# A hybrid attention and MLP block on one core: the bias rows of all 24 heads go to scratch in one DMA with 16 copies each, and a Toeplitz tile is read back by eight DMAs of 16 partitions

## The chip, the cores and the metric

The kernel runs on one core of one Trainium2 chip. The metric is device microseconds of one execution. The kernel before was timed three times: 1610.1, 1610.7 and 1612.06 us, median 1610.7 us.

The core has five engines that run their own instruction streams in order: PE (matmul), DVE (vector), ACT (activation), POOL (GpSimd) and SP, which here only issues DMAs. Sixteen DMA engines move data. Transfers that SP issues appear in the trace as queue q1, those that POOL issues as queue q0.

## The reference, cut to what matters

One decoder layer on 256 tokens of width 2048, all in float32: an RMS norm, one projection of 11,800 columns, three attention mixers A, B and C of eight heads each, a gated sum of their projections, an output projection, and an MLP of width 8192. What the change touches is the relative position bias that every mixer adds to its logits:

```python
def t5_bucket(dist):
    n = jnp.maximum(dist, 0)
    exact = N_BUCKETS // 2
    log_ratio = jnp.log(jnp.maximum(n, 1).astype(jnp.float32) / exact) / math.log(BUCKET_MAX_DIST / exact)
    large = jnp.minimum(exact + (log_ratio * (N_BUCKETS - exact)).astype(jnp.int32), N_BUCKETS - 1)
    return jnp.where(n < exact, n, large)
...
    dist = (jnp.arange(BAND_BLOCK)[:, None] + pad) - jnp.arange(span)[None, :]
    bias = jnp.transpose(bias_tbl[t5_bucket(dist)], (2, 0, 1)).reshape(n_kv, g, BAND_BLOCK, span)
    logits = logits + bias.astype(jnp.float32)
    ...
    p = masked_softmax(logits, mask, sink)
    out = jnp.einsum('bnkgql,bnlkd->bnqkgd', p.astype(v.dtype), vp)
```

The bias of a head depends on the distance query minus key alone. For a tile of 128 queries by 256 keys it is therefore a Toeplitz matrix: each row is the row above it, shifted by one column. All of it is in 383 numbers per head.

## The kernel before, in words

**Dense work.** All weights stream through the core once. `steps` is one list of pieces of weight, each piece 128 partitions by `a` by `b` floats (512 KB for most, 280 KB for the projection of 280 columns called `proj_vw`). For each step `load` issues a DMA from SP into a tile `raw`, `fetch` has ACT round it to `hi` (L79) and DVE take the rest `lo` (L80), and `mm` multiplies both with the activations on PE (L224 to L228 in `dmajor`, L251 to L253 in `tmajor`). The pool `ring` holds four buffers of each of `raw`, `hi` and `lo`.

**Order.** The order is written out by hand: the loop at the end of `hybrid_block` goes through the steps. At step j it runs the step's `pre`, then one slice of the side work in `tasks` (`advance`), then the previous step's evacuation (`late`), then `fetch(j + 3)`, and last the matmuls of step j. So PE has up to three fetched steps ahead of it. But DVE and ACT take their instructions in this order too: the side work of step j+1 stands on DVE behind the `lo` of step j+3, and PE's own side work (transposes, attention) stands between the matmuls of the steps.

**Bias.** `bias_rows`, a task that begins four steps before the end of `proj_vw`, makes `rm`, 24 partitions by 383 floats, one row per head, with the causal mask added. `spread_rows(m)` then writes the eight rows of mixer m into the DRAM tile `scr`, each row 128 times at a pitch of 384 floats (L195). `load_master(m, g)` reads four heads of it at a pitch of 383 floats, so that partition p starts p floats earlier in the row: that is the Toeplitz tile `master`, 128 partitions by 4 heads by 256 keys (L203). There is one buffer for `master`. POOL issues both kinds of DMA, in program order: a `master` load waits for the `scr` write behind it and for DVE's last read of the previous `master` (L450).

`spread_rows(0)` runs in `bias_rows`; `spread_rows(1)` and `spread_rows(2)` run in `start_attn`, when the steps of the first and second branch projection begin to be laid down in the program. POOL reaches them earlier than that place suggests, because it has little else to do. The tile `master` is first read by DVE in `attn_a` (L542, mixer A) and in `core` (L444, mixers B and C).

**Names in the rows.** `cT` and `cs` are a small transpose and its source in `finish`, the end of the block compression; `pt` and `P` are the transposed probabilities in `core`; `fold` is a small constant that POOL's queue copies at the start.

Of the kernel before, what the change touches and what calls it, by code (L numbers as in the profile page):

```python
# [8 lines left out]
F32 = mybir.dt.float32  # L9
# [12 lines left out]
SCALE = 128.0 ** -0.5  # L22
NB = 383
AHEAD = 3

# column offsets in w_in
AQ, AKC, AVC, AKS, AVS, AKW, AVW = 0, 1024, 1280, 1536, 1792, 2048, 2304
BQ, BK, BV = 2584, 3608, 3864
CQ, CK, CV = 4120, 5144, 5400
# [4 lines left out]
def hybrid_block(ctx: ExitStack, tc: tile.TileContext, x, w_in, cmp_pos, cmp_w1, cmp_w2, swa_sinks,  # L34
                 w_branch, w_out, w_mlp_in, w_mlp_out, norm_mix, norm_mlp, norm_final, rel_bias,
                 onehot, rmask, cmask, out):
    nc = tc.nc
# [17 lines left out]
    def pair(name="pair"):  # L55
        return psum.tile([128, 2, 512], F32, name=name, tag="mm")

    # ---------------------------------------------------------------- streamed weights
    steps = []
    tasks = []  # L60

# [3 lines left out]
    loaded = {}  # L65

    def load(j):
        src, a, b = steps[j][:3]
        loaded[j] = ring.tile([128, a, b], F32, name="raw", tag="raw")
        nc.sync.dma_start(loaded[j], src)  # L70

    def fetch(j):
# [19 lines left out]
        while any(t[0] == name for t in tasks):  # L92
            advance()

    # ---------------------------------------------------------------- constants
    xt = bigt([128, 2, D], F32, "xt")

    def load_x(c0, c1):
# [29 lines left out]
    hm = cst.tile([128, 4], F32, name="hm")  # L128
    nc.vector.tensor_reduce(hm, ident.rearrange("p (h c) -> p h c", h=4), axis=AX.X, op=OP.add)

    # ---------------------------------------------------------------- first norm
    part = cst.tile([128, 2, 4], F32, name="part")
    rs = cst.tile([128, 2], F32, name="rs")
    rsh = cst.tile([128, 2], F32, name="rsh")
# [2 lines left out]
    HT = [bigt([128, 8, 512], F32R, f"HT{i}") for i in range(2)]  # L137

    def split_scaled(tiles, k, src, g0):
        """hi and lo parts of two K tiles, src * gain, into columns 0:256 and 256:512."""  # L140
        d = [tiles[(k + a) // 8][:, (k + a) % 8] for a in range(2)]
        g = [gains[:, g0 + k + a:g0 + k + a + 1] for a in range(2)]
        for a in range(2):
            nc.scalar.activation(d[a][:, 0:256], src[:, a], AF.Copy, scale=g[a])
        for a in range(2):
            nc.vector.scalar_tensor_tensor(d[a][:, 256:512], src[:, a], g[a], d[a][:, 0:256].bitcast(F32),
                                           op0=OP.mult, op1=OP.subtract)
# [4 lines left out]
        nc.vector.tensor_copy(gains[:, c0:c0 + n], pc[:, 0:n])  # L152

    def x_block(i):
        """Two K tiles of x * gain; the row factor of the norm follows where products leave PSUM."""
        b = bank("xT").rearrange("p (a q) -> p a q", a=2)
        for a in range(2):
            k = 2 * i + a
            for tt in range(2):
                nc.tensor.transpose(b[:, a, tt * 128:(tt + 1) * 128], xt[:, tt, k * 128:(k + 1) * 128], ident)  # L160
        split_scaled(HT, 2 * i, b, 0)
# [22 lines left out]
    def bias_rows():  # L184
        pr = obank("pr")
        nc.tensor.matmul(pr[0:24, 0:NB], rb, oh, start=True, stop=True)
        nc.vector.tensor_tensor(rm, pr[0:24, 0:NB], rm, op=OP.add)
        yield
        spread_rows(0)
        load_master(0, 0)  # L190
        yield

    def spread_rows(m):
        """Row h 128 times at pitch 384; read at pitch 383 it is a Toeplitz matrix."""
        nc.gpsimd.dma_start(scr[m * 8:(m + 1) * 8, :, 0:NB],  # L195
                            rm[m * 8:(m + 1) * 8, None, :].to_broadcast([8, 128, NB]))

    scr = dram.tile([24, 128, 384], F32, name="scr")
    masters = {}

    def load_master(m, g):
        t = att.tile([128, 4, 256], F32, name="master")
        nc.gpsimd.dma_start(t, bass.AP(tensor=scr.tensor, offset=scr.offset + (m * 8 + g * 4) * 128 * 384 + 127,  # L203
                                       ap=[[383, 128], [128 * 384, 4], [1, 256]]))
        masters[m, g] = t

    # ---------------------------------------------------------------- dense jobs
    def dmajor(w, c0, rhs, evac, kts=KT, pre=None, cuts=(0, 4, 8, 12, 16)):
        """256 columns of w as [column, token]: weights stationary."""
        st = {}  # L210
        for k0, k1 in zip(cuts, cuts[1:]):
            src = w[k0 * 128:k1 * 128, c0:c0 + 256].rearrange("(k p) c -> p k c", p=128)

            def mm(hi, lo, k0=k0, k1=k1):
                if k0 == 0:
                    st["ps"] = pair()
                ps = st["ps"]
                for k in range(k1 - k0):
                    kt = k0 + k
                    r = rhs(kt)  # L220
                    for c in range(2):
                        cs = slice(c * 128, (c + 1) * 128)
                        if kt:
                            nc.tensor.matmul(ps[:, c, 0:256], lo[:, k, cs], r[:, 0:256],  # L224
                                             start=False, stop=False)
                        nc.tensor.matmul(ps[:, c, :], hi[:, k, cs], r, start=kt == 0, stop=kt == kts - 1)  # L226
                        if not kt:
                            nc.tensor.matmul(ps[:, c, 0:256], lo[:, k, cs], r[:, 0:256],  # L228
                                             start=False, stop=False)

            add(src, k1 - k0, 256, mm, pre if k0 == 0 else None,
                (lambda: evac(st["ps"])) if k1 == kts else None)

    def tmajor(w, c0, n, lhs, evac, kts=KT, kc=2, pre=None):
        """n columns of w as [token, column]: activations stationary."""
        st = {}
        for k0 in range(0, kts, kc):
            src = w[k0 * 128:(k0 + kc) * 128, c0:c0 + n].rearrange("(k p) c -> p k c", p=128)

            def mm(hi, lo, k0=k0):  # L240
                if k0 == 0:
                    st["ps"] = pair()
                ps = st["ps"]
                for k in range(kc):
                    kt = k0 + k
                    l = lhs(kt)
                    for tt in range(2):
                        o = ps[:, tt, 0:n]
                        lh = l[:, tt * 128:(tt + 1) * 128]
                        ll = l[:, 256 + tt * 128:256 + (tt + 1) * 128]  # L250
                        nc.tensor.matmul(o, lh, hi[:, k], start=kt == 0, stop=False)  # L251
                        nc.tensor.matmul(o, lh, lo[:, k], start=False, stop=False)  # L252
                        nc.tensor.matmul(o, ll, hi[:, k], start=False, stop=kt == kts - 1)  # L253

            add(src, kc, n, mm, pre if k0 == 0 else None,
                (lambda: evac(st["ps"])) if k0 + kc == kts else None)
# [19 lines left out]
        for tt in range(2):  # L276
            nc.scalar.activation(dst[:, tt], ps[:, tt, c0:c0 + n], func, scale=scale[:, tt:tt + 1])

    # ---------------------------------------------------------------- projections
    w = w_in[0]  # L280
    qT, kT, vt = {}, {}, {}

# [36 lines left out]
            tasks.append(("A", attn_a(1)))  # L319
        tmajor(w, AVW, 280, hT, ev, kc=2)  # L320

    # ---------------------------------------------------------------- compression of blocks
    XH = {}
    kcT = cst.tile([128, 30], F32, name="kcT")
    vcr = cst.tile([128, 2, 128], F32, name="vcr")
# [86 lines left out]
            nc.vector.tensor_copy(vcr, pk[:, 0:256].rearrange("p (g d) -> p g d", g=2))  # L412
        yield

    # ---------------------------------------------------------------- attention
    oT = {}

    def new_o(m):
# [1 line left out]
            oT[m] = bigt([128, 8, 512], F32R, "oT")  # L420

    def core(m, g, q, k, v, o, first, last, gate):
        """Causal attention of the four heads of one kv group; o accumulates [d, (head, token)]."""
        M = masters[m, g]
        h0 = 4 * g
        qp = att.tile([128, 2, 4, 128], F32R, name="qp", tag="P0")
# [154 lines left out]
        store_o(0, g, o)  # L581
        yield

    # ---------------------------------------------------------------- gates and branches
    gt = {}

    def gates(m):
# [26 lines left out]
            tmajor(w_branch[0, m], c * 512, 512, lambda kt: oT[m][:, kt], ev, kts=8, pre=pre)  # L614

    def to_dmajor(src, c, dst, gain0):
        """Column chunk c of a [token, column] tile, transposed and split into hi and lo parts."""
        if not dst:
            dst += [bigt([128, 8, 512], F32R, "dmaj") for _ in range(2)]
        for i in range(2):  # L620
# [12 lines left out]
                split_scaled(dst, k, b, gain0)  # L633
            yield

    # ---------------------------------------------------------------- output projection
    acc = {}
    H2 = []

# [34 lines left out]
        nc.vector.reciprocal(r2, r2)  # L674
        yield

    # ---------------------------------------------------------------- MLP
    hid = {}

    parts = [(4 * i, 4) for i in range(7)] + [(28, 3), (31, 1)]  # L680
# [27 lines left out]
    fin = {}  # L708

    def mlp_last(p):  # L710
        """The last K tiles: the first token tile is done before the second, from the same weights."""
        keep = []
        r0 = parts[p][0] * 256

# [68 lines left out]
            nc.scalar.dma_start(rows[:, 1280:2048], o[:, 1280:2048])  # L783
            nc.sync.dma_start(rows[:, 640:1280], o[:, 640:1280])

    # ---------------------------------------------------------------- order of the work
    def job(f, *a, **kw):
        """The steps of one dense job, taken off the list."""
        n = len(steps)
        f(*a, **kw)  # L790
        r = steps[n:]
        del steps[n:]
        return r
# [29 lines left out]
    n = len(steps)  # L823
# [9 lines left out]

    def start_attn(m, key):
        drain("ABC"[m - 1])
        spread_rows(m)
        load_master(m, 0)
        for g in range(2):
            tasks.append(("ABC"[m], attn(m, g, qT[m], kT[key], vt[key])))
# [12 lines left out]
    n = len(steps)  # L852
# [9 lines left out]
    mlp_last(len(parts) - 1)  # L862
    steps[n - 4] = before(steps[n - 4], load_nf)

    # ---------------------------------------------------------------- emission
    ready = {}
    load_x(0, 256)
    load(0)
# [17 lines left out]
    for j in range(len(steps)):  # L886
# [3 lines left out]
        advance()  # L890
        if late:
            late()
        if j + AHEAD < len(steps):
            ready[j + AHEAD] = fetch(j + AHEAD)
        mm(*ready.pop(j))
# [5 lines left out]


def _constants():
    """Distance buckets and causal masks of the two token tiles: they follow from the shapes alone."""
    import math
    import numpy as np
    dist = 255 - np.arange(NB)
# [28 lines left out]
```

## Time and profile before

| | |
|---|---|
| median of three runs | 1610.7 us (1610.1 to 1612.06) |
| profiled execution, span from first to last instruction | 1610.1 us |
[...]
| PE busy | 1534.5 us, 95% |
| DVE, ACT, POOL busy | 940.4, 718.8, 23.9 us |
| moved by all DMA queues | 298.16 MB, of which POOL's queue 9.33 MB |
| `scr` writes | 3 of 1532 KB, median 36.1 us from issue to landing |
| `master` loads | 6 of 512 KB, median 5.2 us from issue to landing |

PE is the engine that sets the time, so what counts is the time in which it is idle and the time in which it runs at a lower granted clock. The page's 40 slices of about 40 us show both: PE is at 9 tenths or more in most slices, and lower in the first and in slices 4, 7, 8 and 12; the clock line falls in slices 4, 8 and 12. No profile lists anything around the span; the span lies at the lower end of the three times.

### The profile page before, as it was taken

To read this page: it belongs to the slowest core of one execution; us is meant where nothing else is said; L and a number is where in the kernel's file an instruction comes from. 1 tells how busy PE (TensorE), PEld (TensorE's weight loads), DVE (VectorE), ACT (ScalarE), POOL (GpSimd) and SP (SyncE) were. 2 spreads that over 40 slices of the span, in tenths; PEclk is the share of its full clock that TensorE was granted. 3 is DMA by queue.
4 is the path that set the end of the run, shared out by engine and by line. 5 is a ranking of instruction groups with operands and counts; after the bars stand their busy time and mean duration, and the time that the engine had idled before them with its cause. 6 is when DMAs were issued, how large, how long until landed. Compare 5 with 4: busy or idle time off the path is not lost.

```text
span 1610.1 us, 20195 instructions
## 1 busy us (share of the span) xinstructions
PE 1534.5 (95%) x7878; PEld 1305.1 (81%) x7878; DVE 940.4 (58%) x1082; ACT 718.8 (45%) x942; POOL 23.9 (1%) x33
## 2 busy tenths in 40 slices
PE   8995997899959999999999999999999999999997
PEld 7894885688849888888888888888888888888885
DVE  5772663565637547744755666565655566555656
ACT  6551542455524445444445444343434444443443
POOL 1000000000000000000000000000000000000002
PEclk9997999899979999999999999999999999999999
DMA  8696756655666665566655656656565656566563
GB/s 248 193 276 110 223 158 126 174 169 173 176 138 172 183 194 187 168 183 192 225 187 184 188 177 197 192 190 190 186 195 188 193 181 198 181 198 194 189 218 118
DMA packets 211231, 298.16 MB, mean 185 GB/s; under 512 B 10268, under 2 KB 129612, under 8 KB 210752
## 3 DMA queue, kind: packets, MB, share of 16 engines
q1 hardware_dynamic: 207504, 287.15, 58.2%
q0 software_dynamic: 3456, 9.33, 3.8%
q8 instruction: 61, 1.00, 0.3%
q10 hardware_dynamic: 176, 0.40, 0.1%
q14 instruction: 34, 0.28, 0.1%
HBM read 290.02 MB, written 6.80 MB: 184 GB/s over the span
## 4 chain that ended last, share of the span: by engine, by line
PE 90%; DMA 7%; DVE 1%; issue 1%; ACT 1%; POOL 0%; POOLq 0%; DVEq 0%; ACTq 0%
PE pair L226 22%; PE pair L251 17%; PE pair L253 17%; PE pair L252 17%; PE pair L224 11%; DMA raw<-in_w_in_dram 5%; DMA raw<-in_w_branch_dram 2%; PE s L440 1%; PE obank L509 1%; PE pair L228 1%; DVE lo L80 1%; ACT hi L79 1%; PE tm L625 0%; PE obank L512 0%; PE cps L362 0%
## 5 line engine op out<-in xcount | busy, mean ns | idle before, releaser
L80 DVE TENSOR_TENSOR lo<-raw,hi 128x1024 fp32r<-128x1024 f32 (+2 forms) x542 | 653.5, 1213 | 540.1 <-ACT hi L79 538.9
L79 ACT ACTIVATE hi<-raw 128x1024 fp32r<-128x1024 f32 (+2 forms) x542 | 564.3, 1048 | 668.7 <-PE pair L253 385.5
L226 PE MATMUL pair<-dmaj,hi 128*128 128x512 f32 x1024 | 359.8, 398 | 0.0
L224 PE MATMUL pair<-dmaj,lo 128*128 128x256 f32 x960 | 269.7, 281 | 0.0
L226 PEld LDWEIGHTS pair<-dmaj,hi 128*128 128x128 f32 x1024 | 190.8, 188 | 44.5
L226 PE MATMUL pair<-HT,hi 128*128 128x512 f32 x576 | 206.8, 401 | 0.0
L251 PE MATMUL pair<-hi,hid 128*128 128x512 f32 x496 | 192.9, 389 | 0.0
L252 PE MATMUL pair<-lo,hid 128*128 128x512 f32 x496 | 192.9, 389 | 0.0
L253 PE MATMUL pair<-hi,hid 128*128 128x512 f32 x496 | 192.9, 389 | 0.0
L251 PE MATMUL pair<-hi,HT 128*128 128x512 f32 (+2 forms) x512 | 190.0, 371 | 2.7 <-ACT hi L79 2.7
L252 PE MATMUL pair<-lo,HT 128*128 128x512 f32 (+2 forms) x512 | 187.6, 366 | 0.4 <-DVE lo L80 0.4
L253 PE MATMUL pair<-hi,HT 128*128 128x512 f32 (+2 forms) x512 | 187.6, 366 | 0.0
L224 PEld LDWEIGHTS pair<-dmaj,lo 128*128 128x128 f32 x960 | 181.3, 189 | 1.4
L224 PE MATMUL pair<-HT,lo 128*128 128x256 f32 x540 | 153.1, 284 | 2.0 <-DVE lo L80 2.0
L226 PEld LDWEIGHTS pair<-HT,hi 128*128 128x128 f32 x576 | 109.4, 191 | 23.8 <-PE obank L576 0.2
L251 PEld LDWEIGHTS pair<-hi,HT 128*128 128x128 f32 x512 | 98.0, 191 | 17.6 <-ACT hi L79 3.0
L252 PEld LDWEIGHTS pair<-lo,HT 128*128 128x128 f32 x512 | 98.1, 192 | 15.3 <-DVE lo L80 0.6
L253 PEld LDWEIGHTS pair<-hi,HT 128*128 128x128 f32 x512 | 98.0, 191 | 15.3
L252 PEld LDWEIGHTS pair<-lo,hid 128*128 128x128 f32 x496 | 93.1, 188 | 19.4
L253 PEld LDWEIGHTS pair<-hi,hid 128*128 128x128 f32 x496 | 93.1, 188 | 19.4
L251 PEld LDWEIGHTS pair<-hi,hid 128*128 128x128 f32 x496 | 93.1, 188 | 18.9
L224 PEld LDWEIGHTS pair<-HT,lo 128*128 128x128 f32 x540 | 103.0, 191 | 3.1 <-DVE lo L80 2.2
(211 smaller groups left out, 1354.2 us busy)
## 6 DMA issues: line engine op xcount, KB each, us to landing
raw<-in_w_in_dram SPq DMA_DIRECT2D x178, 512.0 KB, 3.8
raw<-in_w_mlp_in_dram SPq DMA_DIRECT2D x128, 512.0 KB, 3.9
raw<-in_w_mlp_out_dram SPq DMA_DIRECT2D x128, 512.0 KB, 4.4
raw<-in_w_branch_dram SPq DMA_DIRECT2D x48, 512.0 KB, 4.4
raw<-in_w_out_dram SPq DMA_DIRECT2D x32, 512.0 KB, 4.4
raw<-in_cmp_w_dram SPq DMA_DIRECT2D x16, 512.0 KB, 4.6
scr<-rm POOLq DMA_DIRECT2D x3, 1532.0 KB, 36.1
master<-scr POOLq DMA_DIRECT2D x6, 512.0 KB, 5.2
```

The lines of the kernel that those rows point to most:

```text
L79: nc.scalar.activation(hi, raw, AF.Copy)
L80: nc.vector.tensor_tensor(lo, raw, hi.bitcast(F32), op=OP.subtract)
L224: nc.tensor.matmul(ps[:, c, 0:256], lo[:, k, cs], r[:, 0:256], start=False, stop=False)
L226: nc.tensor.matmul(ps[:, c, :], hi[:, k, cs], r, start=kt == 0, stop=kt == kts - 1)
L228: nc.tensor.matmul(ps[:, c, 0:256], lo[:, k, cs], r[:, 0:256], start=False, stop=False)
L251: nc.tensor.matmul(o, lh, hi[:, k], start=kt == 0, stop=False)
L252: nc.tensor.matmul(o, lh, lo[:, k], start=False, stop=False)
L253: nc.tensor.matmul(o, ll, hi[:, k], start=False, stop=kt == kts - 1)
L440: nc.tensor.matmul(b[:, h], qp[:, a, 2 * i + h], kp[:, c], start=n == 0, stop=n == 2)
L509: nc.tensor.matmul(ob, v[:, a, 0, g * 128:(g + 1) * 128], P0[c][:, hs], start=first and n == 0, stop=False, skip_group_check=True)
```

## The change

The rows of all 24 heads are written at once, in `bias_rows`, each 16 times in place of 128; `spread_rows` is gone and with it the two later writes. A copy at pitch 384 read at pitch 383 shifts by one float per partition, and 16 copies serve 16 partitions; so `load_master` issues eight DMAs, each for 16 partitions, with the starting column moved back by 16 from one to the next. A few comments are dropped, and the main loop gets a second loop that would issue raw loads earlier if `RAWS` were larger than `AHEAD + 1`; with `RAWS = 4` and `AHEAD = 3` its range is empty.

```diff
 AHEAD = 3
+RAWS = 4
...
-        loaded[j] = ring.tile([128, a, b], F32, name="raw", tag="raw")
+        loaded[j] = ring.tile([128, a, b], F32, name="raw", tag="raw", bufs=RAWS)
...
         nc.vector.tensor_tensor(rm, pr[0:24, 0:NB], rm, op=OP.add)
         yield
-        spread_rows(0)
+
+        nc.gpsimd.dma_start(scr[:, :, 0:NB], rm[:, None, :].to_broadcast([24, RB, NB]))
         load_master(0, 0)
         yield
 
-    def spread_rows(m):
-        """Row h 128 times at pitch 384; read at pitch 383 it is a Toeplitz matrix."""
-        nc.gpsimd.dma_start(scr[m * 8:(m + 1) * 8, :, 0:NB],
-                            rm[m * 8:(m + 1) * 8, None, :].to_broadcast([8, 128, NB]))
-
-    scr = dram.tile([24, 128, 384], F32, name="scr")
+    RB = 16
+    scr = dram.tile([24, RB, 384], F32, name="scr")
     masters = {}
 
     def load_master(m, g):
         t = att.tile([128, 4, 256], F32, name="master")
-        nc.gpsimd.dma_start(t, bass.AP(tensor=scr.tensor, offset=scr.offset + (m * 8 + g * 4) * 128 * 384 + 127,
-                                       ap=[[383, 128], [128 * 384, 4], [1, 256]]))
+        for a in range(128 // RB):
+            nc.gpsimd.dma_start(
+                t[a * RB:(a + 1) * RB],
+                bass.AP(tensor=scr.tensor, offset=scr.offset + (m * 8 + g * 4) * RB * 384 + 127 - a * RB,
+                        ap=[[383, RB], [RB * 384, 4], [1, 256]]))
         masters[m, g] = t
...
     def start_attn(m, key):
         drain("ABC"[m - 1])
-        spread_rows(m)
         load_master(m, 0)
...
+        for i in range(j + AHEAD, min(j + RAWS - 1, len(steps))):
+            if i not in loaded and i not in ready:
+                load(i)
         if j + AHEAD < len(steps):
             ready[j + AHEAD] = fetch(j + AHEAD)
```

On POOL this is the stretch from the bias rows to the last norm, before; a row gives the line, the operation, the tile written and read, and the shape (1024x1x383 is 1024 rows of 383 floats):

```order
L172 TENSOR_TENSOR rs<-rs,nhalf 128x2
L195 DMA scr<-rm 1024x1x383
L203 DMA master<-scr 128x4x256
L540 MEMSET Lc 128x256
L203 DMA master<-scr 128x4x256
L540 MEMSET Lc 128x256
L195 DMA scr<-rm 1024x1x383
L203 DMA master<-scr 128x4x256 x2
L195 DMA scr<-rm 1024x1x383
L203 DMA master<-scr 128x4x256 x2
```

And the same stretch in the changed kernel, where the lines are numbered one lower or higher:

```order
L173 TENSOR_TENSOR rs<-rs,nhalf 128x2
L191 DMA scr<-rm 384x1x383
L202 DMA master<-scr 16x4x256 x8
L541 MEMSET Lc 128x256
L202 DMA master<-scr 16x4x256 x8
L541 MEMSET Lc 128x256
L202 DMA master<-scr 16x4x256 x32
```

Three writes of 1024 rows have become one of 384, six loads have become 48, and `Lc`'s two memsets now stand behind eight loads each in place of one.

On DVE nothing moves, but the first reader of a `master` waits for more. These are the rows around the first read in `attn_a`, before, with the semaphores that each waits for (DMASW are those of POOL's DMAs, DMAHW those of SP's):

```order
L80 TENSOR_TENSOR lo<-raw,hi 128x1024 [waits DMAHW0_49,DVE_49,Activation_49]
L542 SCALAR_TENSOR_TENSOR Lc<-sc,master 128x4x15 [waits DMASW2_49,PE_49,Pool_49]
L544 SCALAR_TENSOR_TENSOR Lc<-sc,master 128x4x7
L548 TENSOR_REDUCE nm<-Lc 128x8 [waits DVE_49]
L80 TENSOR_TENSOR lo<-raw,hi 128x1024 [waits DMAHW1_49,Activation_49]
```

And in the changed kernel:

```order
L81 TENSOR_TENSOR lo<-raw,hi 128x1024 [waits DMAHW0_49,DVE_49,Activation_49]
L543 SCALAR_TENSOR_TENSOR Lc<-sc,master 128x4x15 [waits DMASW3_49,DMASW4_49,DMASW2_49,DMASW5_49,DMASW1_49,DMASW6_49,DMASW0_49,DMASW7_49,PE_49,Pool_49]
L545 SCALAR_TENSOR_TENSOR Lc<-sc,master 128x4x7
L549 TENSOR_REDUCE nm<-Lc 128x8 [waits DVE_49]
L81 TENSOR_TENSOR lo<-raw,hi 128x1024 [waits DMAHW1_49,Activation_49]
```

The one semaphore of the `master` load has become eight; the order on DVE is the same, as it is on PE, ACT and SP throughout.

## Rows read from the trace of the kernel before

**Rows 1.** The page: span, and PE's busy time, share and instructions.
```profile
span 1610.1 us, 20195 instructions
PE 1534.5 (95%) x7878; PEld 1305.1 (81%) x7878; DVE 940.4 (58%) x1082; ACT 718.8 (45%) x942; POOL 23.9 (1%) x33
```

**Rows 2.** Waits of PE, whole span: us in total, times, longest.
```profile
PE pt L501 <- DVE P L494: 37.0, 2, 18.9
PE cT L378 <- DVE cs L372: 17.9, 1, 17.9
...
PE pair L251 <- ACT hi L79: 2.7, 1, 2.7
```

**Rows 3.** Chain that ended last: start us, us, what; the first of three.
```profile
129.90 33.39 DMA raw<-in_w_in_dram
```

**Rows 4.** Timeline of POOL: start us, us, line, what, [idle before <- releaser].
```profile
6.13 0.52 POOL L883 DMA_DIRECT2D fold<-ident  x1
...
128.01 1.15 POOL L195 DMA_DIRECT2D scr<-rm  x1 [83.20 <-DVE rm L187]
163.37 0.78 POOL L203 DMA_DIRECT2D master<-scr  x1 [34.21 <-DMA raw<-in_w_in_dram]
...
252.15 0.76 POOL L203 DMA_DIRECT2D master<-scr  x1 [87.67 <-DVE L L450]
...
432.84 0.75 POOL L203 DMA_DIRECT2D master<-scr  x1 [52.91 <-DVE L L450]
433.58 1.11 POOL L195 DMA_DIRECT2D scr<-rm  x1
...
619.37 0.75 POOL L203 DMA_DIRECT2D master<-scr  x1 [124.42 <-DVE L L450]
```

**Rows 5.** Source views of L195, then L203: their DMAs from issue to landing.
```profile
DMA to landing us min/median/max: 35.1/36.1/37.5
...
DMA to landing us min/median/max: 4.2/5.2/6.4
```

**Rows 6.** DMA queues in 145 to 155 us: packets, MB, share of 16 engines.
```profile
q0 software_dynamic: 107, 0.49, 47.8%
q1 hardware_dynamic: 106, 0.11, 3.1%
```

**Rows 7.** Timelines of ACT, DVE and PE from 155 to 157.5 us.
```profile
155.38 0.67 ACT L79 ACTIVATE hi<-raw 128x560 fp32r<-128x560 f32 x1 [19.97 <-DMA raw<-in_w_in_dram]
...
156.74 0.41 DVE L372 COPY cs<-cps 60x256 f32<-60x256 f32 x1
...
157.30 0.39 PE L378 MATMUL cT<-fold,cs 60*128 60x30 f32 x1 [17.89 <-DVE cs L372]
```

**Rows 8.** Windows: length; PE, PEld, DVE, ACT, POOL busy (x); PEclk, DMA share, GB/s.
```profile
157.30:161.40 4.10, 4.10 (x16) 3.72 (x16) 0.00 (x0) 0.00 (x0) 0.00 (x0) 0.50 0.63 94
...
164.10:169.50 5.40, 5.01 (x24) 4.79 (x25) 4.78 (x14) 2.27 (x4) 0.37 (x2) 0.68 0.91 281
288.80:292.00 3.20, 3.20 (x11) 2.73 (x12) 0.52 (x1) 0.53 (x1) 0.00 (x0) 0.57 0.79 236
468.50:472.50 4.00, 4.00 (x12) 3.33 (x13) 2.60 (x3) 1.82 (x2) 0.00 (x0) 0.50 0.74 264
320.00:400.00 80.00, 80.00 (x385) 66.52 (x383) 47.92 (x67) 42.21 (x76) 0.77 (x1) 1.00 0.61 173
```

**Rows 9.** Readers of `master`: the tile view (first and last start), then DVE's timeline.
```profile
L542 DVE SCALAR_TENSOR_TENSOR Lc<-sc,master x2: 249/250/252, 181.0 to 306.0; 128x60 f32<-128x60 f32 x2
...
489.03 1.28 DVE L444 SCALAR_TENSOR_TENSOR L<-s,master 128x512 f32<-128x512 f32 x2
...
655.43 1.28 DVE L444 SCALAR_TENSOR_TENSOR L<-s,master 128x512 f32<-128x512 f32 x2
```

**Rows 10.** DVE's semaphore waits ahead of L444: ns min/median/max.
```profile
L444 DVEq EVENT_SEMAPHORE  x4: 21/21/21, 426.6 to 654.3; - x4
```

**Rows 11.** DMA issues on POOL, 1 to 8 us: KB each, us to landing.
```profile
fold<-ident POOLq DMA_DIRECT2D x1, 3.5 KB, 7.3
```

## The prediction, made before the changed kernel ran

> **What bounds the kernel now.** First the page: PE is busy 1534.5 of 1610.1 us [rows 1], so the time is PE's, and only PE's idle time and a lower clock can be won. Next the waits of PE: of the 75.6 us that it is idle, 57.6 us stand in four waits [rows 2], two of `pt` on DVE (37.0 us, the longer 18.9, so the other 18.1), one of `cT` on DVE (17.9) and one of a `pair` on ACT (2.7). DVE is named, but it is only the last link. The rows of the first wait show why [rows 7]: the raw piece lands, ACT takes it up at 155.38 after 19.97 us of waiting for that DMA, DVE's `cs` follows behind the `lo` of the same piece at 156.74, and PE goes on at 157.30. So PE, which had fetched steps ahead, stood still for a small copy queued on DVE behind a piece of weight that had not come. The chain of waits says the same: it runs through a raw DMA of 33.39 us at 129.90 [rows 3], the first of three such.
>
> Why was the piece late? POOL's timeline has a `scr` write at 128.01 and another at 433.58 [rows 4], and such a write is 35.1 to 37.5 us under way [rows 5]; the second of the three lies between them, behind the `master` load of 252.15. Each stall falls into one of these. The queues in the middle of the first write, 145 to 155 us [rows 6]: q0 has 47.8% of 16 engines, or 7.6 engines, and with q1's 3.1% about 8.1 engines are at work. There are eight source rows of `rm`. q0's 107 packets hold 0.49 MB, so three rows of 1532 bytes each, and take 0.478 x 160 / 107 = 0.715 us; q1's 106 packets take 0.031 x 160 / 106 = 0.047 us. One packet of weight passes for each packet of the write, 0.762 us a pair, on the eight engines that the write holds, and a raw piece is complete only when its share on those engines is through.
>
> After each stall PE also works at a lower clock. [...] PE's busy time there times the missing part of the clock is 2.05, 1.60, 1.38 and 2.00 us.
>
> So the three stalls cost: first 17.9 + 2.7 + 2.05 + 1.60 = 24.2 us; second 18.9 + 1.38 = 20.3; third 18.1 + 2.0 = 20.1. Together 64.6 us.
>
> **The second and third write** go away entirely. What is left at those places is a `master` load of as many bytes as before. A stretch with such a load and no write is 320 to 400 us: POOL issues one DMA, PE is busy 80.00 of 80 us at clock 1.00 [rows 8]. I take all of both stalls, 40.4 us; what could be late next there is a `master`, below.
>
> **The first write** stays at its place but has 384 rows in place of 1024. Before, an engine had 128 rows, 42.7 packets, times 0.762 = 32.5 us; of the 35.1 us to landing [rows 5] 2.6 are left for start and end. The trace doesn't show on how many engines 24 source rows go. If still eight, an engine has 48 rows, 16 pairs, 12.2 us, and the write lands after 14.8; if all sixteen, 24 rows, 8 pairs, 6.1 us, landing after 8.7. That is at 136.7 to 142.8 us; I take the middle, 139.7, as the two ends are equally near. The raw piece that came at 155.38 needed most of 25 us of one-for-one service, so I let it land with the write. PE followed 157.30 - 155.38 = 1.9 us later [rows 7], and ran dry at 157.30 - 17.89 = 139.4. So it stands still until 141.6, 2.2 us, with ends 0 (138.6, before it runs dry) and 5.3 (144.7). Before, an idle stretch of 2.7 us was followed by a slow one that cost 1.60; I add 1.6, and at the far end the old 2.05 + 1.60. The first stall shrinks from 24.2 to 3.8 us (0 to 9.0): 20.4 us won (15.2 to 24.2).
>
> [...]
>
> **The eight loads per `master`.** POOL issues 48 in place of 6. One issue took 0.75 to 0.78 us for 512 KB, and 0.52 us for the small `fold` [rows 4]; eight take 4.2 to 6.2 us, and the last lands 4.2 to 6.4 us after its own issue [rows 5], so a `master` is complete 8 to 13 us after its first issue in place of 4 to 6. Who waits? DVE in L542 and L444. From issue to first read there are 306.0 - 252.15 = 53.9 us, 489.03 - 432.84 = 56.2 and 655.43 - 619.37 = 36.1 [rows 4, 9]; the first two lose a stall each in between, leaving 33.6 and 36.1. The loads of mixers B and C that are issued before their attention starts have more. The tightest is the very first: issued at 140.0, complete by 153 at the latest, read at 181.0 - 20.4 = 160.6. So all are covered, with 8 us to spare at the worst; without cover each microsecond is lost in full, since DVE is in order and PE's transposes hang on it. `Lc`'s memset stands behind the eight issues on POOL and is late by 3 to 5 us, with the same reader and the same cover. DVE waits for seven semaphores more per `master`, 21 ns each [rows 10]: 7 x 6 x 21 ns = 0.9 us, beside PE's work while DVE is busy 58% [rows 1]. The new loop over `RAWS` is empty and costs nothing.
>
> [...]
>
> **Sum.** 20.4 + 20.3 + 20.1 = 60.8 us off the profiled 1610.1 gives 1549.3; the median of the runs is 0.6 above that execution, so 1550. With the ends of the first write: 1546 to 1555.
>
> **Rivals.**
> *The first write is not shorter.* If its 35 us were set by something that doesn't shrink with the rows (one slow engine, or more engines held for the raw pieces), the first stall would stay: 1610.7 - 40.4 = 1570, and part of it would give 1555 to 1570. Against it: 42.7 pairs times 0.762 explain 32.5 of the 35.1 us.
> *The stalls are not the write's.* If the `master` load in the same place delayed the raw pieces, stalls two and three would stay, 1590. Against it: the full PE in 320 to 400 us.
> *The eight loads run one after another (the other side).* Then a `master` takes eight times 4.2 to 6.4 us [rows 5], 34 to 51, against 20.6, 33.6, 36.1 and 36.1 us until its read. At c us per load the lateness is 32c - 126.4: at 5.2 us 40, so 1590; at 6.4 us 78, so 1628. From c = 5.9 on it eats all 60.8 us and the kernel is slower. For it: all eight go through POOL's one queue. Against it: `fold`, the last of nine loads that POOL issues back to back at the start, is issued at 6.13 and lands 7.3 us later, at 13.4 [rows 4, 11]; nine in a row at 4.2 us each would need 38.
>
> **How the numbers follow.** Forecast, 1546 to 1555: 76%. First stall mostly kept, 1555 to 1571: 10%. Loads in a row but below the turning point, or stalls two and three kept, 1571 to 1607: 8%. In a row above it: 5%. Nothing: 1%. The range 1543 to 1562 takes in the forecast, half of the first rival, and a little below the 1546 at which all three stalls are gone. A difference under 0.2% (3 us) can't be told from none. Faster 94%, within 1%, slower 5%.
>
> **What would show it.** Right: no PE wait over 6 us after the start of the kernel; the clock at 1.00 around 270 and 440 us; one `scr` write that lands in 9 to 15 us; POOL's issues eight at a time at 0.5 to 0.8 us; no DVE idle time ended by a `master`. Wrong: a `cT` wait near 18 us (the first rival), `pt` waits of 18 us (the second), or DVE idle ahead of L542 or L444 until a `master` lands (the third).

## The result and the profile after

The changed kernel takes 1545.16 us (median of four runs, 1544.38 to 1545.77), against 1610.86 us for the kernel before on the same chip: ratio 0.9595, 95% interval 0.9582 to 0.9609. That is 65.7 us less, 60.8 were forecast; the time lies in the range, 5 us under the predicted 1550 and just under the 1546 at which, by the forecast's count, all three stalls are gone.

The page of the changed kernel, span, busy times and the clock line:

```profile
span 1542.6 us, 20262 instructions
...
PE 1525.0 (99%) x7878; PEld 1297.7 (84%) x7878; DVE 940.5 (61%) x1082; ACT 718.9 (47%) x942; POOL 41.0 (3%) x73
...
PEclk9999999999999999999999999999999999999999
```

Against [rows 1] PE's idle time went from 75.6 to 17.6 us, 58.0 less, and its busy time from 1534.5 to 1525.0, 9.5 less with the same 7878 instructions, at a mean granted clock of 0.998 in place of 0.978 (1 is full speed). Together that is the whole 67.5 us between the spans. Of the 9.5 us some 1.6 are not the change's: from 10 to 30 us, before any bias row exists, the granted clock was 0.91 in the profile of before and 1.00 in this one, with 18 us of work. The next two rows show that, first before, then after (columns as in [rows 8]):

```profile
10.00:30.00 20.00, 18.00 (x99) 15.71 (x98) 12.74 (x19) 11.02 (x18) 0.00 (x0) 0.91 0.94 294
```

```profile
10.00:30.00 20.00, 18.06 (x110) 15.82 (x109) 13.62 (x22) 12.71 (x22) 0.00 (x0) 1.00 0.98 302
```

The waits of PE over the whole span, all that there are (compare [rows 2]):

```profile
PE pc L152 <- DMA mix_rows<-in_norm_mix_dram: 3.5, 1, 3.5
PE pair L225 <- DVE lo L81: 1.9, 1, 1.9
PE xT L161 <- DMA xt<-in_x_dram: 1.3, 2, 0.9
```

All three belong to the start of the kernel. The waits of `pt` and `cT` are gone, and the windows around the former stalls show PE full at clock 1.00:

```profile
133.00:140.00 7.00, 7.00 (x55) 6.80 (x55) 5.16 (x11) 2.75 (x5) 3.17 (x7) 1.00 0.97 245
140.00:150.00 10.00, 10.00 (x77) 9.57 (x75) 7.36 (x15) 6.37 (x11) 0.00 (x0) 1.00 0.95 281
220.00:260.00 40.00, 40.00 (x204) 33.90 (x203) 25.11 (x38) 20.07 (x36) 4.36 (x9) 1.00 0.62 174
380.00:430.00 50.00, 50.00 (x248) 42.22 (x248) 36.33 (x51) 24.93 (x48) 7.75 (x16) 1.00 0.63 184
```

POOL's timeline (compare [rows 4]): one write, then loads eight at a time, 4.03 to 4.06 us for eight issues (once 4.33, with a gap after the first).

```profile
125.42 0.75 POOL L191 DMA_DIRECT2D scr<-rm  x1 [82.65 <-DVE rm L188]
131.80 4.06 POOL L202 DMA_DIRECT2D master<-scr  x8 [5.62 <-DMA scr<-rm]
...
224.83 4.03 POOL L202 DMA_DIRECT2D master<-scr  x8 [87.08 <-DVE L L451]
```

The write is 6.1 us from issue to landing, where 8.7 was the lower bound. Each load of 64 KB takes 2.5 to 5.3 us. These are the landings in the source views of the write and of the loads (compare [rows 5]):

```profile
DMA to landing us min/median/max: 6.1/6.1/6.1
```

```profile
DMA to landing us min/median/max: 2.5/3.6/5.3
```

ACT, DVE and PE at the place of the first stall (compare [rows 7]): ACT takes up the piece of weight at 132.73 without waiting for a DMA, DVE's `lo` of the same piece and then `cs` follow, and PE's `cT` has no idle time before it.

```profile
132.73 0.66 ACT L80 ACTIVATE hi<-raw 128x560 fp32r<-128x560 f32 x1
...
134.20 0.73 DVE L81 TENSOR_TENSOR lo<-raw,hi 128x560 fp32r<-128x560 f32 x1
134.85 0.41 DVE L373 COPY cs<-cps 60x256 f32<-60x256 f32 x1
...
136.75 0.63 PE L379 MATMUL cT<-fold,cs 60*128 60x30 f32 x4
```

Why the write was so much shorter than its bound is in the queues, 128.2 to 130.2 us (compare [rows 6]; columns are packets, MB, share of 16 engines):

```profile
q0 software_dynamic: 62, 0.28, 74.6%
q1 hardware_dynamic: 96, 0.10, 17.3%
```

A packet of the write, again three rows, takes 0.746 x 32 / 62 = 0.385 us (16 engines times 2 us are 32), where a packet of the same size took 0.715 us before. The forecast held this number fixed. That is what the experiments had to settle, beside the shares of the three parts of the change.

### The profile page after: what moved, and what is told of

The parts are those of the page before. It is cut to its first block, busy times and chain, and to the rows that moved or that the text cites. A ratio compares the mean times of both kernels' runs of the same rounds, so it can differ in the third digit from the quotient of the medians.

```text
span 1542.6 us, 20262 instructions
## 1 busy us (share of the span) xinstructions
PE 1525.0 (99%) x7878; PEld 1297.7 (84%) x7878; DVE 940.5 (61%) x1082; ACT 718.9 (47%) x942; POOL 41.0 (3%) x73
## 3 DMA queue, kind: packets, MB, share of 16 engines
q1 hardware_dynamic: 207504, 287.15, 60.8%
## 4 chain that ended last, share of the span: by engine, by line
PE 98%; DMA 1%; POOL 0%; issue 0%; DVE 0%; ACT 0%; POOLq 0%; DVEq 0%; ACTq 0%
PE pair L227 24%; PE pair L252 19%; PE pair L254 19%; PE pair L253 19%; PE pair L225 11%; PE s L441 1%; PE pair L229 1%; PE obank L510 1%; DMA raw<-in_w_in_dram 1%; PE tm L626 0%; PE cps L363 0%; PE cps L362 0%; PE s L449 0%; PE pt L487 0%; PE obank L513 0%
## 5 line engine op out<-in xcount | busy, mean ns | idle before, releaser
L225 PE MATMUL pair<-dmaj,lo 128*128 128x256 f32 x960 | 269.9, 281 | 0.0
L225 PEld LDWEIGHTS pair<-dmaj,lo 128*128 128x128 f32 x960 | 181.4, 189 | 1.3
L225 PE MATMUL pair<-HT,lo 128*128 128x256 f32 x540 | 152.1, 282 | 1.9 <-DVE lo L81 1.9
L252 PEld LDWEIGHTS pair<-hi,HT 128*128 128x128 f32 x512 | 96.5, 188 | 14.6 <-issue 0.2
L225 PEld LDWEIGHTS pair<-HT,lo 128*128 128x128 f32 x540 | 102.1, 189 | 3.0 <-DVE lo L81 2.2
```

## The experiments

**One write of all rows, still 128 copies.** The kernel before with the later writes gone and the loads as they were:

```diff
-        spread_rows(0)
+        nc.gpsimd.dma_start(scr[:, :, 0:NB], rm[:, None, :].to_broadcast([24, 128, NB]))
...
-        spread_rows(m)
```

> The kernel before with one part of the change alone: all 24 rows are written at once at the start, but each still 128 times, and each master is one DMA. The two later writes are gone, so by every theory the second and third stall are gone: 40 us. What the first write of 4.7 MB does tells the theories apart. Theory P (a packet's time is set by how many DMA engines read source rows out of the same four neighbouring partitions: four before, two with 24 rows on 12 engines): packets of 0.37 us as in the changed kernel, 256 rows an engine are 85 pairs of 0.42 us, landing after about 38 us, a first stall about as long as before (20 to 30 us), time 1565 to 1575. Theory F (the forecast's: 0.715 us a packet, whatever the source): 85 pairs of 0.762, landing after 67 us, a first stall of 50 us or more, time 1595 to 1605. Theory C (packets are short only because each row is copied 16 times in place of 128): as F.

Measured: 1569.34 us, ratio to before 0.9752 (0.9734 to 0.9771). The waits of PE behind the write, and the queues from 135 to 155 us, in the middle of it:

```profile
PE vc L409 <- DVE gr L402: 11.2, 1, 11.2
PE pair L251 <- ACT hi L79: 6.2, 2, 3.3
```

```profile
q0 software_dynamic: 615, 2.83, 67.1%
q1 hardware_dynamic: 972, 1.01, 16.1%
```

The packets take 0.671 x 320 / 615 = 0.349 us although every row is copied 128 times: theory P's number, not F's or C's. Counted in pairs with a packet of weight, as in the prediction, 615 packets in 20 us at 0.349 + 0.053 us a pair are an estimated 12.4 engines at work. The write lands after 37.0 us, as forecast by P. The first stall of this kernel, with PE's clock, is the 24.2 us by which it is slower than the changed one (24.1 against the next run, which was timed with it). Dropping the two later writes brought the other 39.9; the first stall changed too, though: PE is idle 11.2 + 6.2 + 0.8 us there, where it was 17.9 + 2.7 + 0.4 before.

**Sixteen copies, but three writes.** The other part alone, with the eight loads that it needs:

```diff
-                            rm[m * 8:(m + 1) * 8, None, :].to_broadcast([8, 128, NB]))
+                            rm[m * 8:(m + 1) * 8, None, :].to_broadcast([8, 16, NB]))
```

> The other part of the change alone: three writes of eight rows, each at its old place, but 16 copies each, and eight DMAs per master. Eight engines, 16 rows each, 5.3 packets. Theories P and F: packets stay at about 0.72 us, as eight rows lie in two groups of four partitions; landing after 2.6 + 5.3 x 0.76 = 6.7 us. Theory C: packets of 0.37 us, landing after 4.8 us. All three: no PE stall at any of the three writes, time within 2 us of the changed kernel, 1544 to 1547: then the number of copies alone carries the whole gain, and writing once adds nothing.

Measured: 1545.24 us, ratio 0.9601 (0.9586 to 0.9616). No PE wait behind the start. The queues during the first write, 130.3 to 132.3 us:

```profile
q0 software_dynamic: 19, 0.09, 43.8%
q1 hardware_dynamic: 129, 0.14, 22.7%
```

0.438 x 32 / 19 = 0.738 us a packet: with eight neighbouring source rows packets are long again, with 16 copies as with 128, which ends theory C. But an engine has only an estimated 5.3 of them (128 rows, three to a packet, on eight engines); the write lands after 6.1 us (median), and nobody waits. The number of copies alone carries the whole gain; writing once adds nothing to it that these runs can tell.

**The same 128 copies from source rows further apart.** Nothing of the change is in these two. The row of head h is made in partition 2h, then 4h, of `rm` (PP is 2, then 4; the lines that fill `rbs`, the bias table spread the same way, are left out):

```diff
-    rm = att.tile([24, NB], F32, name="rm", tag="hu")
-    nc.gpsimd.dma_start(rm, rmask)
+    rm = att.tile([24 * PP, NB], F32, name="rm", tag="hu")
+    nc.gpsimd.memset(rm, 0.0)
+    nc.gpsimd.dma_start(rm[0:24 * PP:PP], rmask)
+    rbs = cst.tile([32, 24 * PP], F32, name="rbs")
...
-                            rm[m * 8:(m + 1) * 8, None, :].to_broadcast([8, 128, NB]))
+                            rm[m * 8 * PP:(m + 1) * 8 * PP:PP, None, :].to_broadcast([8, 128, NB]))
```

> The kernel before, 128 copies and three writes, with the row of head h in partition 2h of rm in place of h, so that eight source rows lie in four groups of four partitions and two engines share a group. Theory P: packets of about 0.37 us, 42.7 pairs of 0.42 us, landing after 18 to 21 us, each stall shorter by 14 to 15 us (3 to 5 us left of each, less clock loss), time 1560 to 1575. Theories F and C: packets of 0.72 us, landing after 35 us, time 1608 to 1613.

> As the kernel before with the row of head h in partition 4h of rm: eight source rows in eight groups, one engine each. Theory P: packets of 0.17 to 0.25 us (the master loads' 4 KB packets are the nearest row), 42.7 pairs, landing after 12 to 16 us, stalls of 0 to 2 us left at each write, time 1546 to 1553: nearly the whole gain of the change with not one copy fewer. Theories F and C: no change, 1608 to 1613.

Measured: 1564.96 us for a pitch of two (0.9722, 0.9705 to 0.974) and 1547.99 us for a pitch of four (0.9618, 0.9603 to 0.9634). The write's packets, first at a pitch of two, 130 to 140 us, then at four, 131 to 133 us:

```profile
q0 software_dynamic: 206, 0.95, 44.4%
```

```profile
q0 software_dynamic: 72, 0.33, 40.0%
```

0.444 x 160 / 206 = 0.345 us, and 0.400 x 32 / 72 = 0.178 us. Destination, copies and bytes are those of the kernel before; only the partitions of the source differ. The number of engines at work, counted in pairs again (q1's packets in the same views: 546 at 19.0%, 0.056 us each, and 145 at 29.3%, 0.065 us), is an estimated 8.3 and 8.7, where 107 pairs of 0.762 us in 10 us [rows 6] give 8.2 before. Landing fell from 36.1 to 20.9 and 14.6 us (medians). What is left of the waits of PE behind the start at a pitch of two, and at four:

```profile
PE pt L505 <- DVE P L498: 8.2, 2, 5.0
...
PE pair L255 <- ACT hi L79: 2.5, 1, 2.5
PE cT L382 <- DVE cs L376: 2.3, 1, 2.3
```

```profile
PE vc L413 <- DVE gr L406: 1.4, 1, 1.4
```

So 61 of the 66 us can be had without one copy fewer.

**Only the eight loads.** The kernel before, 128 copies and three writes, with each `master` read by eight DMAs:

```diff
-        nc.gpsimd.dma_start(t, bass.AP(tensor=scr.tensor, offset=scr.offset + (m * 8 + g * 4) * 128 * 384 + 127,
-                                       ap=[[383, 128], [128 * 384, 4], [1, 256]]))
+        for a in range(8):
+            nc.gpsimd.dma_start(
+                t[a * 16:(a + 1) * 16],
+                bass.AP(tensor=scr.tensor, offset=scr.offset + (m * 8 + g * 4) * 128 * 384 + 127 + a * 16 * 383,
+                        ap=[[383, 16], [128 * 384, 4], [1, 256]]))
```

> The kernel before with the third part of the change alone: three writes of 128 copies as before, and each master read by eight DMAs of 16 partitions. If the eight loads are covered (the forecast's reading): 1608 to 1612, the same three stalls. If issuing or landing of eight loads is dearer than 5.9 us each: later by the lateness, 1630 or more. A second thing is open: at the second and third place the write stands on POOL behind the eight issues, so it starts about 3.3 us later than before, and the stalls move with it without growing.

Measured: 1615.43 us against 1611.4, ratio 1.003 (1.002 to 1.004): 4 us slower, above the 1608 to 1612 expected and far from 1630. The waits of PE:

```profile
PE obank L512 <- ACT P L496: 38.6, 2, 20.3
PE cT L381 <- DVE cs L375: 11.4, 1, 11.4
PE pair L254 <- ACT hi L79: 7.8, 1, 7.8
...
PE obank L512 <- DVE P L497: 1.2, 2, 0.6
```

The stalls at the second and third write are 38.6 + 1.2 = 39.8 us in place of 37.0 [rows 2]. The write stands behind the eight issues there and starts 4.3 and 4.0 us after the first of them, by POOL's timeline, where it started 1.0 and 0.7 us after the one load before; that the stalls also grow by 2.8 us was not expected, and why is not settled. No wait on a `master` load shows. In the changed kernel, where no write follows the loads, there is no stall for this to lengthen.

**One write, 64 copies.** The changed kernel with a longer write, to see what a waiting piece of weight waits for:

```diff
-    RB = 16
+    RB = 64
```

> The changed kernel with 64 copies in place of 16 (two loads of 64 partitions per master): 128 rows an engine on 12 engines, 42.7 pairs. By the packets of 0.35 to 0.39 us that 24 source rows have shown, a pair takes 0.40 to 0.43 us and the write lands after 19 to 21 us. Theory L (the forecast's step: the waiting weight piece is complete only with the write): piece at 146 to 148, PE dry from 137.5 to 139.4 and on again 1.9 us after the piece, idle 10 us, with the clock 1557 to 1561. Theory R (one weight packet passes for each packet of the write, so a 280 KB piece of 16 packets an engine comes every 16 pairs, 6.5 us, during the write): first late piece at 137 to 139 and the next at 144, idle 4 to 6 us, 1550 to 1554.

Measured: 1555.09 us, ratio 0.965 (0.9636 to 0.9664). The pieces of weight as ACT takes them up, then the waits of PE at the write:

```profile
139.35 0.67 ACT L80 ACTIVATE hi<-raw 128x560 fp32r<-128x560 f32 x1 [4.00 <-DMA raw<-in_w_in_dram]
...
145.95 0.67 ACT L80 ACTIVATE hi<-raw 128x560 fp32r<-128x560 f32 x1 [5.93 <-DMA raw<-in_w_in_dram]
```

```profile
PE pair L252 <- ACT hi L80: 2.2, 1, 2.2
PE cT L379 <- DVE cs L373: 1.9, 1, 1.9
...
PE pair L253 <- DVE lo L81: 0.2, 1, 0.2
```

The write was issued at 127.95 and landed after 19.4 us, at 147.3; two pieces came before that, 6.6 us apart, which is an estimated 16 pairs of 0.41, both a little later than R had them. PE was idle 4.3 us: theory R, not L's 10. The time is 1 us above R's range. The clock at the write cost an estimated 4.2 us: in 133 to 150 and 150 to 160 us it was 0.78 and 0.86, with 12.66 and 9.97 us of work, 2.8 + 1.4. But the profiled execution is the slowest of the four (1555.6 us at a mean granted clock of 0.993; the fastest took 1554.67 us at 0.996), and the `pair` wait of L225 is 3.1 us in it, 1.9 in the changed kernel; what makes the difference of 1 us is not shown.

```profile
133.00:150.00 17.00, 12.66 (x74) 11.54 (x73) 4.49 (x8) 3.39 (x6) 1.56 (x3) 0.78 0.82 200
150.00:160.00 10.00, 9.97 (x63) 9.40 (x63) 6.57 (x16) 4.71 (x7) 0.00 (x0) 0.86 1.00 290
```

The same is seen with 128 copies in one write. These are four pieces on ACT while that write was under way:

```profile
142.77 0.67 ACT L79 ACTIVATE hi<-raw 128x560 fp32r<-128x560 f32 x1 [8.31 <-DMA raw<-in_w_in_dram]
149.42 0.67 ACT L79 ACTIVATE hi<-raw 128x560 fp32r<-128x560 f32 x1 [5.99 <-DMA raw<-in_w_in_dram]
156.01 0.67 ACT L79 ACTIVATE hi<-raw 128x560 fp32r<-128x560 f32 x1 [5.92 <-DMA raw<-in_w_in_dram]
162.58 0.67 ACT L79 ACTIVATE hi<-raw 128x560 fp32r<-128x560 f32 x1 [5.91 <-DMA raw<-in_w_in_dram]
```

A piece comes every 6.6 us: pieces pass at the pace of the write's packets, and these are half as long as before (0.349 us, 0.715 before). That would explain why this write, which lands as late as the ones before (37.0 us, median 36.1 before), costs PE less idle time (11.2 + 6.2 us, against 17.9 + 2.7 in [rows 2]); in the kernel before one late piece came, at 155.38, before its write had landed. What these rows do not explain is the first late piece: before, it was issued at 129.2 and took 26.1 us, 34 pairs of 0.762, and with 64 copies it was at ACT 11.4 us after the write's issue, an estimated 28 pairs of 0.41, where the later ones took 16.

## Why the prediction was right, point by point

- **What the time was lost to.** Right. The three stalls and the low clock behind them (0.50 to 0.68 in the first four windows of [rows 8]) were the `scr` writes': with the writes shortened in any of three ways (fewer copies, source rows apart, fewer writes) they shrink or go, and the places where a `master` load alone stood in their stead show a full PE at clock 1.00 (40.00 of 40 us and 50.00 of 50). The rival by which the `master` loads were to blame has fallen.
- **Second and third stall, 40.4 us.** Right: the 37.0 us of `pt` waits are gone, and 39.9 us lie between the kernel before and the one that only drops the later writes, with a first stall that is some 3 us shorter in idle time.
- **First write, 20.4 us won of 24.2.** The mechanism was right, the term was mis-sized: all 24.2 are won, nothing is left of the stall. The write was put at 11.7 us from issue to landing (139.7 - 128.01) and took 6.1, under the 9 to 15 that the prediction named as a sign of being right. Two numbers were off, both to the same side. The packet of 0.715 us was taken to stay as it was; it is that of eight neighbouring source rows on an estimated 8.1 engines, and with 24 it is 0.385. The number of engines was left between 8 and 16 and the middle of the two landings taken; the run with one write of 128 copies gives an estimated 12.4. With 12, an engine has an estimated 10.7 pairs of 0.385 + 0.058 us (q1: 0.173 x 32 / 96), 4.7 us, and 1.4 are left for start and end. The waiting piece was let land with the write. In the changed kernel that came out: the piece was issued at 126.3, landed 5.9 us later, at 132.2, and the write at 131.5. As a rule it is wrong: with 64 copies the piece was at ACT 8 us before the write landed. Either way it now is at ACT 7.3 us after the write's issue, and PE would have run dry only 11.4 us after it (139.4 - 128.01).
- **Eight loads, no cost.** Right in the changed kernel: eight issues take 4.03 to 4.06 us (4.2 to 6.2 forecast), a `master` is complete at most 4.33 + 5.3 = 9.6 us after its first issue (8 to 13), the first is read 20 us after it, and no wait on one shows. One after another, at the 2.5 us of the shortest, eight would take an estimated 20 us (8 x 2.5); the loads overlap. This is the read, from DVE's timeline:

```profile
151.84 0.25 DVE L543 SCALAR_TENSOR_TENSOR Lc<-sc,master 128x60 f32<-128x60 f32 x1
```

- **The sum.** 60.8 forecast, 65.7 measured by the medians. Its clock terms (2.05, 1.60, 1.38 and 2.00 us) are PE's busy time in the first four windows of [rows 8] times the part of full speed that their granted clocks of 0.50, 0.68, 0.57 and 0.50 lack. The difference is the 3.8 us of the first stall and about 1 us that the sizes of the clock loss and of single runs leave open. One step of the sum compared unlike things: it put the median 0.6 us above the profiled execution by taking the span for that execution's time. The changed kernel's profiled execution took 1544.38 us with a span of 1542.6; by that difference the profiled execution before, with a span of 1610.1, took an estimated 1612 us and lay above the median. It changes little, as 60.8 off the median of 1610.7 is 1550 as well.
- **The other side.** Loads in a row from 5.9 us each: not so, eight are done within 9.6.

## What to carry to other kernels

A short side transfer can starve the main stream if it holds a few DMA engines for long (here 1.57 MB, an estimated 8.1 of the 16 engines for 36.1 us): look at the queue's packets, share and landing, not at its bytes, and at who stands in order behind the piece that is late. Before cutting the bytes, ask from how many partitions the transfer reads and how far apart they are; here a pitch of four in the source was worth 61 us by itself. And a packet time read from one transfer did not hold here for another with more source rows or rows further apart: 0.715 us became 0.385 and 0.349, 0.345 and 0.178 for packets of the same size.

## What the runs showed of the hardware

The time of a 4.6 KB packet from `rm` to DRAM followed the partitions that the source rows lie in, and not the number of copies. With eight rows in neighbouring partitions it was 0.715 us for 128 copies (before) and 0.738 us for 16; with eight rows in every second partition 0.345, in every fourth 0.178; with 24 rows in neighbouring partitions 0.349 us for 128 copies and 0.385 for 16 (the changed kernel). That is theory P, an estimated 0.18 us for each engine that reads from the same four partitions, if the rows are shared out evenly: 0.715 / 4, 0.345 / 2, 0.349 / 2 and 0.178 / 1. Which engine reads which partition no trace shows, nor that the group is of four partitions: groups of eight would have twice as many engines in each of these runs, and give the same four times with half of it for each. The packet of 0.178 us may be an engine's own limit as well.

On the engines that two queues share, one packet of the one passed for one packet of the other: 106 against 107 in the middle of the first write before [rows 6], with an estimated 8.1 engines at work. Under the single writes of 64 and 128 copies a piece of weight, an estimated 16 packets on an engine (256 runs of 280 floats over 16 engines), came every 6.6 us, which is an estimated 0.41 us a pair; with 128 copies 0.349 + 0.053 = 0.402 us were read from the queues.
